# The third row pair of the gate and up weights in seven products, with one weight sum made by an adding DMA

## Chip, cores and metric

The kernel runs on one core of one Trainium2 chip. The metric is the device time of one execution in microseconds (us); of the kernel before it is 2270.07 us, the median of 3 runs (2270.04 to 2271.07).

## What is computed

A trunk of four pre-norm residual layers over 256 tokens of width 2048: a gated linear recurrence (HGRN2) or gated linear attention (GLA), each with cross-attention into 256 memory tokens and an output projection, and after each of the two a SwiGLU feed-forward layer. Everything is float32. The part around the change is the feed-forward layer, the largest by weights (D_FF is 5632):

```python
hn = _rmsnorm(h, norm_ffn[layer])
gate, up = jnp.split(hn @ w_gate_up[layer], 2, axis=-1)
h = h + (jax.nn.silu(gate) * up) @ w_down[layer]
```

## The kernel before

**Products.** A float32 product is made of two float32r parts of each factor: `split` (L276) writes a weight's high part with ScalarE (a rounded copy) and its low part, the rest, with VectorE. A "product" is then three matmuls of 128x512 into one PSUM bank: high x high, high x low, low x high.

**Row pairs and kinds.** The 2048 rows of a weight are 8 row pairs of 2 x 128 rows. For a pair and two blocks of 512 columns (in the feed-forward layer one of gate and one of up) there are four weight tiles, two rows by two columns, and the 256 tokens are two halves of 128. So each pair is a 2 x 2 block product. A pair's kind says how it is made:

- `S` (`seven`, L420): seven products in the manner of Strassen and Winograd, 21 matmuls. It needs weight sums on VectorE, and parts of four sums beside those of three tiles: parts `a` (one tile of 512), `b`, `c` and `d` (two tiles, 1024, each).
- `O`: eight products, 24 matmuls, on the four weight tiles as they are (parts `a` and `b`) and on differences of the token factors.
- `H`: eight products, 24 matmuls, with the token factors that `S` has; it needs one weight difference and its parts.

The token factors are made once in each layer, in `Forms` (L359), by the kind of the pair in `PAIRS` (L354): "S" pairs get eight of them, "O" six. `project_halves` (L591) goes through the eight pairs of a block of gate and up columns with the kinds of `KINDS` (L1161). There are 11 such blocks a layer; the blocks 0 to 3 have rows of their own there and the blocks 4 to 10, here called steady, the last row. The same `load_pair` and `seven` serve the "S" pairs of the other projections (`project_two`, L516, for the memory keys and values, HGRN2, GLA, the output projection and the last two quads of the down weights).

**Order of work.** Between two gate/up blocks run two pieces of the down projection (`fd` in the profile), each over two quads (four row tiles, one load of 1024 KB each). The weights go through `raw` tiles of four 128x512 slots, with 3 buffers (`new_raw`, L271), loaded by SyncE's DMA queue in the order of use; a load waits until the last reader of the tile three before it, as a rule VectorE's last low part, is done. The parts go through tiles of tag `parts` with 6 buffers: an `S` pair takes three of them and one of tag `part`, an `O` pair or a quad two. So VectorE can work ahead of TensorE by that much. From the fourth pair of each layer's first gate/up block on, the instructions of TensorE, VectorE and ScalarE are kept in the order in which the program issues them (`Engine.kept`); `mark` and `due` put the sums of the last block, the gate and the transposes at fixed places in it. In each block of the feed-forward layer but the first, one low part of the down weights is written by GpSimd in place of VectorE (`free_port`, L286).

**An `S` pair on VectorE.** The low parts of `a` and `b`, then one sum of 1024 columns and two of 512, then the low parts of `c` and `d`. TensorE uses them in the order that the lists in `project_halves` give (`(1, 3, 2, 5, 7, 6, 4)`, and in the block's last pair `(1, 2, 6, 7, 5, 4, 3)`): product 1 is of `a`, 2 and 3 of `b`, 5 and 7 of `c`, 6 and 4 of `d`.

In the profile nearly every instruction of TensorE, VectorE and ScalarE has line L151, a helper that issues it, so that one reads by the tiles: `raw` (weights as loaded, and their sums), `parts143d` (parts d of raw tile 143), `f_p` (banks of a gate/up block), `fd` (banks of the down projection), `hf_7h` and `hf_7l` (token factors of pair 7, high and low). The three matmuls of a product with one stationary factor appear as a row of x2 (high factor) and one of x1 (low factor).

Of the kernel before, what the change touches and what calls it, by code (L numbers as in the profile page):

```python
# [17 lines left out]
P = 128  # L18
# [22 lines left out]
def trunk_kernel(ctx: ExitStack, tc: tile.TileContext, x, mem, norm_mix, norm_ffn, norm_mem,  # L41
# [234 lines left out]
    def split(src, name, by=2):  # L276
# [6 lines left out]
        for k in range(0, n, by):  # L283
            j = min(k + by, n)
            ac.copy(out=both[:, 0, k:j, 0:m], in_=src[:, k:j, :])
# [68 lines left out]
    PAIRS = "SSOSSOSB"  # L354
# [4 lines left out]
    class Forms:  # L359
# [20 lines left out]
        def put(self, ps, gains):  # L380
# [11 lines left out]
            if self.kind == "O":  # L392
# [3 lines left out]
            ve.scalar_tensor_tensor(out=g[:, 4, :], in0=g[:, 0, :], scalar=-1.0, in1=g[:, 3, :],  # L396
                                           op0=ALU.mult, op1=ALU.subtract)
            tt(out=g[:, 5, :], in0=g[:, 1, :], in1=g[:, 0, :], op=ALU.subtract)
            tt(out=g[:, 6, :], in0=g[:, 3, :], in1=g[:, 5, :], op=ALU.subtract)
            tt(out=g[:, 7, :], in0=g[:, 2, :], in1=g[:, 6, :], op=ALU.subtract)  # L400
# [7 lines left out]
    def load_pair(raw, w, p, c0, c1, n):  # L408
# [7 lines left out]
        for j, c in ((slice(0, 4, 3), c0), (slice(1, 3), c1)):  # L416
            nc.sync.dma_start(out=raw[:, j, 0:n],
                              in_=w[2 * p * P:(2 * p + 2) * P, c:c + n].rearrange("(k p) c -> p k c", p=P))

    def seven(i, raw, between=None):  # L420
# [8 lines left out]
        tt(out=raw[:, 0:2, :], in0=raw[:, 0:4:2, :], in1=raw[:, 1:2, :].broadcast_to([P, 2, n]), op=ALU.subtract)  # L429
        tt(out=raw[:, 2, :], in0=raw[:, 2, :], in1=raw[:, 0, :], op=ALU.add)  # L430
        tt(out=raw[:, 3, :], in0=raw[:, 3, :], in1=raw[:, 2, :], op=ALU.subtract)
        t5, t7 = split(raw[:, 0:2, :], f"{i}c")
        t6, t4 = split(raw[:, 2:4, :], f"{i}d")
        return {1: ("x00", b00), 2: ("x01", b10), 3: ("z", b11), 4: ("x11", t4), 5: ("s", t5), 6: ("u", t6), 7: ("d0", t7)}

    def further(g):

        tt = ve.tensor_tensor
        ve.scalar_tensor_tensor(out=g[:, 4, :], in0=g[:, 1, :], scalar=-1.0, in1=g[:, 3, :], op0=ALU.mult, op1=ALU.subtract)
        tt(out=g[:, 5, :], in0=g[:, 0, :], in1=g[:, 1, :], op=ALU.subtract)  # L440
        tt(out=g[:, 6, :], in0=g[:, 3, :], in1=g[:, 5, :], op=ALU.subtract)
        tt(out=g[:, 7, :], in0=g[:, 2, :], in1=g[:, 6, :], op=ALU.subtract)
# [73 lines left out]
    def project_two(pairs, plan, w, c0, c1, n, name, give, view=lambda ps: ps, onto=None, prep=None, behind=None,  # L516
# [43 lines left out]
        for at, (p, kind) in enumerate(zip(order, plan)):  # L560
            i, raw = new_raw()
            if i == 0:
                load_pair(raw, w, p, c0, c1, n)
            if prep:
                prep(at)
            if i > 0:
                load_pair(raw, w, p, c0, c1, n)
            if kind == "S":
                todo = held(behind, seven, i, raw[:, :, 0:n]) if behind else seven(i, raw[:, :, 0:n])
                last = at == plan.rindex("S")  # L570
                for b in (1, 6, 7, 5, 2, 4, 3) if last else (3, 2, 1, 5, 7, 6, 4):
# [817 lines left out]
```

## Time and profile before

| | |
|---|---|
| median of 3 runs | 2270.07 us |
| the profiled execution's own time | 2271.69 us |
| its span, first to last instruction | 2269.9 us |
| granted TensorE clock | 0.999 |
| TensorE busy | 2250.8 us |
| VectorE busy | 2065.8 us |
| ScalarE busy | 1423.5 us |
| GpSimd busy | 83.4 us |
| moved by DMA | 435.78 MB |

The profile is of one execution. PE is TensorE, DVE VectorE, ACT ScalarE, POOL GpSimd, SP SyncE with its DMA queue. A row of a group of instructions has: line, engine, operation, output and inputs by tile, shapes and type, count; behind the first bar the busy time in us and the mean of one in ns; behind the second the idle time of the engine before them, and who ended it. A window's row has, for each engine, the busy time in it and the number of instructions, then the granted clock, the share of time in which the DMA engines were busy, and GB/s.

### The profile page before, as it was taken

What the parts mean: (1) busy time and instruction counts of PE and PEld (TensorE: products, weight loads), DVE (VectorE), ACT (ScalarE), POOL (GpSimd) and SP (SyncE); (2) the same over time, 40 slices, a digit from 0 to 9 for tenths busy, and PEclk for the clock granted to TensorE, in tenths of its full rate; (3) what the DMA queues carried; (4) which work ended last, traced back from release to release, by engine and by line L of the source; (5) the groups of instructions that cost most, each with busy time, mean ns of one, the idle gap of its engine ahead of it and who ended that gap; (6) DMA issues with size and microseconds to landing.
All of it is one profiled execution on the core that took longest, in us unless ns stands there. A gap on an engine that the chain in (4) does not pass through costs nothing.

```text
span 2269.9 us, 29374 instructions
## 1 busy us (share of the span) xinstructions
PE 2250.8 (99%) x10710; PEld 1901.4 (84%) x10710; DVE 2065.8 (91%) x2615; ACT 1423.5 (63%) x1938; POOL 83.4 (4%) x61
## 2 busy tenths in 40 slices
PE   9999999999999999999999999999999999999998
PEld 7888888888888888888889999988888888888887
DVE  7889999899999999999996887899899999999997
ACT  6655656566666666666665665566566666666664
POOL 0000000000000000000000000001000000000000
PEclk9999999999999999999999999999999999999999
DMA  8645545455556665555665446555556565665564
GB/s 289 204 151 183 186 157 177 167 168 203 170 202 222 204 206 190 203 199 204 204 212 174 142 146 190 157 176 203 197 194 203 205 210 194 205 205 202 205 217 153
DMA packets 232644, 435.78 MB, mean 192 GB/s; under 512 B 13199, under 2 KB 42675, under 8 KB 232243
## 3 DMA queue, kind: packets, MB, share of 16 engines
q1 hardware_dynamic: 231203, 429.64, 56.4%
q10 hardware_dynamic: 1296, 4.26, 0.5%
q8 instruction: 84, 1.38, 0.2%
q14 instruction: 61, 0.50, 0.1%
HBM read 430.71 MB, written 3.15 MB: 191 GB/s over the span
## 4 chain that ended last, share of the span: by engine, by line
PE 89%; DVE 6%; ACT 2%; issue 1%; DMA 1%; POOL 0%; SPq 0%; POOLq 0%; DVEq 0%; ACTq 0%
PE f_p L151 39%; PE fd L151 19%; PE wo L151 4%; PE m1p L151 2%; PE wo0p L151 2%; PE hf0p L151 2%; PE wo1p L151 2%; PE fd_0p L151 2%; PE gk1p L151 1%; PE gg11p L151 1%; PE gg10p L151 1%; PE gg01p L151 1%; PE m0p L151 1%; DVE raw L151 1%; PE gx L151 1%
## 5 line engine op out<-in xcount | busy, mean ns | idle before, releaser
L151 DVE TENSOR_TENSOR raw<-raw 128x512 f32<-128x512 f32 (+3 forms) x474 | 403.6, 852 | 9.2
L151 ACT CAST parts<-raw 128x1024 fp32r<-128x1024 f32 (+1 forms) x216 | 212.0, 1016 | 44.6 <-DMA raw<-in_w_down_dram 9.8
L151 DVE TENSOR_TENSOR parts<-raw,parts 128x1024 fp32r<-128x1024 f32 (+1 forms) x196 | 224.0, 1180 | 15.2 <-ACT parts L151 15.1
L286 POOL TENSOR_TENSOR parts<-raw,parts 128x1024 fp32r<-128x1024 f32 x20 | 48.2, 2411 | 1187.1 <-ACT parts L151 1138.6
L151 ACT COPY h<-fd 128x512 f32<-128x512 f32 x80 | 46.3, 588 | 55.0 <-PE fd L151 52.1
L151 ACT ACTIVATE s<-s,rf_r 128x512 f32<-128x512 f32 x44 | 31.8, 722 | 41.6 <-DVE s L151 41.4
L151 DVE TENSOR_TENSOR e<-f_p,e 128x512 f32<-128x512 f32 x66 | 45.2, 685 | 2.3
L151 ACT COPY fd<-h 128x512 f32<-128x512 f32 x82 | 45.2, 582 | 0.0
L151 PE MATMUL fd<-parts,s_6h 128*128 128x512 f32 x128 | 39.8, 392 | 0.0
L151 PE MATMUL fd<-parts,s_8h 128*128 128x512 f32 x128 | 39.8, 392 | 0.0
L151 PE MATMUL fd<-parts,s_4h 128*128 128x512 f32 x128 | 39.8, 392 | 0.0
L151 PE MATMUL fd<-parts,s_2h 128*128 128x512 f32 x128 | 39.8, 392 | 0.0
L151 PE MATMUL fd<-parts,s_0h 128*128 128x512 f32 x128 | 39.8, 392 | 0.0
L151 PE MATMUL fd<-parts,s_5h 128*128 128x512 f32 x128 | 39.4, 389 | 0.0
L151 PE MATMUL fd<-parts,s_3h 128*128 128x512 f32 x128 | 39.4, 389 | 0.0
L151 PE MATMUL fd<-parts,s_7h 128*128 128x512 f32 x128 | 39.4, 389 | 0.0
L151 PE MATMUL fd<-parts,s_1h 128*128 128x512 f32 x128 | 39.4, 389 | 0.0
L151 DVE TENSOR_TENSOR s<-f_p,e 128x512 f32<-128x512 f32 x44 | 30.3, 689 | 4.3 <-PE f_p L151 2.4
L151 DVE SCALAR_TENSOR_TENSOR s<-e,rf_r,s 128x512 f32<-128x512 f32 x44 | 31.0, 747 | 0.2
L151 PEld LDWEIGHTS fd<-parts,s_7h 128*128 128x128 f32 x128 | 24.0, 188 | 5.0
L151 PEld LDWEIGHTS fd<-parts,s_3h 128*128 128x128 f32 x128 | 24.0, 188 | 5.0
L151 PEld LDWEIGHTS fd<-parts,s_1h 128*128 128x128 f32 x128 | 24.0, 188 | 5.0
(5723 smaller groups left out, 7258.1 us busy)
## 6 DMA issues: line engine op xcount, KB each, us to landing
raw<-in_w_gate_up_dram SPq DMA_DIRECT2D x352, 512.0 KB, 3.9
raw<-in_w_down_dram SPq DMA_DIRECT2D x80, 1024.0 KB, 5.7
raw<-in_hgrn_w_in_dram SPq DMA_DIRECT2D x96, 512.0 KB, 3.9
raw<-in_gla_w_in_dram SPq DMA_DIRECT2D x96, 384.0 KB, 3.3
raw<-in_w_out_dram SPq DMA_DIRECT2D x16, 1024.0 KB, 5.8
raw<-in_w_out_dram SPq DMA_DIRECT2D x32, 512.0 KB, 4.1
raw<-in_w_mem_kv_dram SPq DMA_DIRECT2D x30, 512.0 KB, 5.5
raw<-in_w_down_dram SPq DMA_DIRECT2D x16, 512.0 KB, 4.1
```

The lines of the kernel that those rows point to most:

```text
L151: ins = func(*args, **kwargs)
L286: low = (nc.gpsimd if free_port else ve).tensor_tensor(out=both[:, 1, k:j, 0:m], in0=src[:, k:j, :], in1=both[:, 0, k:j, 0:m].bitcast(F32) ...
```

## The change

In steady blocks pair 2 becomes an `S` pair (`PAIRS` and the last row of `KINDS`): seven `S` and one `O` in place of six and two. As its token factors are now those of `S`, it becomes `H` in the blocks 0 to 3 of each layer, where it was `O`.

In all `S` pairs of the kernel, the weight sum of slot 1 (the upper row's second column block plus the lower row's) is no longer made by VectorE: after the two loads of the pair, which change places, GpSimd issues a DMA that reads the lower row's tile (128x512, or 128x384 in GLA) from DRAM once more and adds it onto slot 1 (`accum_op=ALU.add`). There are 168 of these. The signs of the sums change to suit: VectorE then makes one sum of 512 columns and one of 1024, parts `c` are now those of the products 6 and 7 and are written negated (`turned`: ScalarE's copy with scale -1, VectorE's low part by a scalar_tensor_tensor), parts `d` are those of 5 and 4. The token sums (`Forms.put`, `further`) change sign alike, and the order of the products becomes `(1, 3, 2, 6, 7, 5, 4)`; in the last pair it stays as it was in numbers, but 6 is now of `c` and 5 of `d`. The diff:

```diff
--- before.py
+++ after.py
@@ -273,7 +273,7 @@
         n_w[0] += 1
         return i, wts.tile([P, 4, 512], F32, tag="raw", name=f"raw{i}", bufs=3)
 
-    def split(src, name, by=2):
+    def split(src, name, by=2, turned=False):
 
         n, m = src.shape[1:]
         if n == 1:
@@ -282,6 +282,12 @@
             both = wts.tile([P, 2, 2, 512], F32R, tag="parts", name=f"parts{name}", bufs=6)
         for k in range(0, n, by):
             j = min(k + by, n)
+            if turned:
+                hi = both[:, 0, k:j, 0:m]
+                ac.activation(out=hi, in_=src[:, k:j, :], func=AF.Copy, scale=-1.0)
+                ve.scalar_tensor_tensor(out=both[:, 1, k:j, 0:m], in0=src[:, k:j, :], scalar=-1.0, in1=hi.bitcast(F32),
+                                        op0=ALU.mult, op1=ALU.subtract)
+                continue
             ac.copy(out=both[:, 0, k:j, 0:m], in_=src[:, k:j, :])
             low = (nc.gpsimd if free_port else ve).tensor_tensor(
                 out=both[:, 1, k:j, 0:m], in0=src[:, k:j, :], in1=both[:, 0, k:j, 0:m].bitcast(F32), op=ALU.subtract)
@@ -351,7 +357,7 @@
 
 
 
-    PAIRS = "SSOSSOSB"
+    PAIRS = "SSSSSOSB"
     HOMES = (("hq", "hq"),) * 4 + (("F", "K"), ("T", "sc"), ("Q", None), ("v", "gate"))
     FACTORS = {"S": ("x10", "x00", "x01", "x11", "s", "d0", "u", "z"), "O": ("x10", "x00", "x01", "x11", "d0", "d1"),
                "B": ("x10", "x00", "x01", "x11", "s", "d0", "u", "z", "d1")}
@@ -393,11 +399,10 @@
                 tt(out=g[:, 4:6, :], in0=g[:, 1:3, :], in1=g[:, 0:4:3, :], op=ALU.subtract)
                 parts(0, 0, 6)
                 return
-            ve.scalar_tensor_tensor(out=g[:, 4, :], in0=g[:, 0, :], scalar=-1.0, in1=g[:, 3, :],
-                                           op0=ALU.mult, op1=ALU.subtract)
-            tt(out=g[:, 5, :], in0=g[:, 1, :], in1=g[:, 0, :], op=ALU.subtract)
-            tt(out=g[:, 6, :], in0=g[:, 3, :], in1=g[:, 5, :], op=ALU.subtract)
-            tt(out=g[:, 7, :], in0=g[:, 2, :], in1=g[:, 6, :], op=ALU.subtract)
+            tt(out=g[:, 4:6, :], in0=g[:, 3:0:-2, :], in1=g[:, 0:1, :].broadcast_to([P, 2, P]), op=ALU.subtract)
+            ve.scalar_tensor_tensor(out=g[:, 6, :], in0=g[:, 3, :], scalar=-1.0, in1=g[:, 5, :],
+                                    op0=ALU.mult, op1=ALU.subtract)
+            tt(out=g[:, 7, :], in0=g[:, 2, :], in1=g[:, 6, :], op=ALU.add)
             parts(0, 0, 8)
             if self.kind == "B":
                 tt(out=g[:, 4, :], in0=g[:, 2, :], in1=g[:, 3, :], op=ALU.subtract)
@@ -405,7 +410,7 @@
 
     TIMES = {"S": (1,) * 7, "O": (0, 2, 2, 2, 2, 0, 0), "H": (0, 2, 2, 2, 1, 0, 1)}
 
-    def load_pair(raw, w, p, c0, c1, n):
+    def load_pair(raw, w, p, c0, c1, n, kind):
 
         if n_w[0] == 1:
             for k, j, c in ((0, 0, c0), (0, 1, c1), (1, 3, c0), (1, 2, c1)):
@@ -413,9 +418,11 @@
                 if k == 0 and c == c1:
                     load_mem(0, 256, 512)
             return
-        for j, c in ((slice(0, 4, 3), c0), (slice(1, 3), c1)):
+        for j, c in ((slice(1, 3), c1), (slice(0, 4, 3), c0)):
             nc.sync.dma_start(out=raw[:, j, 0:n],
                               in_=w[2 * p * P:(2 * p + 2) * P, c:c + n].rearrange("(k p) c -> p k c", p=P))
+        if kind == "S":
+            nc.gpsimd.dma_start(out=raw[:, 1, 0:n], in_=w[(2 * p + 1) * P:(2 * p + 2) * P, c1:c1 + n], accum_op=ALU.add)
 
     def seven(i, raw, between=None):
 
@@ -426,20 +433,19 @@
         if between:
             between()
 
-        tt(out=raw[:, 0:2, :], in0=raw[:, 0:4:2, :], in1=raw[:, 1:2, :].broadcast_to([P, 2, n]), op=ALU.subtract)
-        tt(out=raw[:, 2, :], in0=raw[:, 2, :], in1=raw[:, 0, :], op=ALU.add)
-        tt(out=raw[:, 3, :], in0=raw[:, 3, :], in1=raw[:, 2, :], op=ALU.subtract)
-        t5, t7 = split(raw[:, 0:2, :], f"{i}c")
-        t6, t4 = split(raw[:, 2:4, :], f"{i}d")
+        tt(out=raw[:, 0, :], in0=raw[:, 1, :], in1=raw[:, 0, :], op=ALU.subtract)
+        tt(out=raw[:, 2:4, :], in0=raw[:, 2:4, :], in1=raw[:, 0:1, :].broadcast_to([P, 2, n]), op=ALU.subtract)
+        t6, t7 = split(raw[:, 0:2, :], f"{i}c", turned=True)
+        t5, t4 = split(raw[:, 2:4, :], f"{i}d")
         return {1: ("x00", b00), 2: ("x01", b10), 3: ("z", b11), 4: ("x11", t4), 5: ("s", t5), 6: ("u", t6), 7: ("d0", t7)}
 
     def further(g):
 
         tt = ve.tensor_tensor
-        ve.scalar_tensor_tensor(out=g[:, 4, :], in0=g[:, 1, :], scalar=-1.0, in1=g[:, 3, :], op0=ALU.mult, op1=ALU.subtract)
+        tt(out=g[:, 4, :], in0=g[:, 3, :], in1=g[:, 1, :], op=ALU.subtract)
         tt(out=g[:, 5, :], in0=g[:, 0, :], in1=g[:, 1, :], op=ALU.subtract)
-        tt(out=g[:, 6, :], in0=g[:, 3, :], in1=g[:, 5, :], op=ALU.subtract)
-        tt(out=g[:, 7, :], in0=g[:, 2, :], in1=g[:, 6, :], op=ALU.subtract)
+        ve.scalar_tensor_tensor(out=g[:, 6, :], in0=g[:, 3, :], scalar=-1.0, in1=g[:, 5, :], op0=ALU.mult, op1=ALU.subtract)
+        tt(out=g[:, 7, :], in0=g[:, 2, :], in1=g[:, 6, :], op=ALU.add)
 
     class Pair:
 
@@ -560,15 +566,15 @@
         for at, (p, kind) in enumerate(zip(order, plan)):
             i, raw = new_raw()
             if i == 0:
-                load_pair(raw, w, p, c0, c1, n)
+                load_pair(raw, w, p, c0, c1, n, kind)
             if prep:
                 prep(at)
             if i > 0:
-                load_pair(raw, w, p, c0, c1, n)
+                load_pair(raw, w, p, c0, c1, n, kind)
             if kind == "S":
                 todo = held(behind, seven, i, raw[:, :, 0:n]) if behind else seven(i, raw[:, :, 0:n])
                 last = at == plan.rindex("S")
-                for b in (1, 6, 7, 5, 2, 4, 3) if last else (3, 2, 1, 5, 7, 6, 4):
+                for b in (1, 6, 7, 5, 2, 4, 3) if last else (3, 2, 1, 6, 7, 5, 4):
                     product(b, pairs[p].get(todo[b][0]), todo[b][1])
                 if last and at == len(plan) - 1:
                     early()
@@ -607,12 +613,12 @@
         for p, kind in enumerate(kinds):
             Engine.kept = keep <= p
             i, raw = new_raw()
-            load_pair(raw, w, p, c0, c1, 512)
+            load_pair(raw, w, p, c0, c1, 512, kind)
             x = forms[p].get
             last = p == len(PAIRS) - 1
             if kind == "S":
                 todo = seven(i, raw, lambda: mark(key + p))
-                for b in (1, 2, 6, 7, 5, 4, 3) if last else (1, 3, 2, 5, 7, 6, 4):
+                for b in (1, 2, 6, 7, 5, 4, 3) if last else (1, 3, 2, 6, 7, 5, 4):
                     product(b, x(todo[b][0]), todo[b][1])
             else:
                 b00, b01 = split(raw[:, 0:2, :], f"{i}a")
@@ -1158,7 +1164,7 @@
     PARTS = ((0,), (1, 2), (3, 4), (5, 6), (7, 8), (9, 10))
 
 
-    KINDS = ("SHOSHOSO", "HHOSSOSO", "SHOSSOSO", "SSOSSOHS", "SSOSSOSS")
+    KINDS = ("SHHSHOSO", "HHHSSOSO", "SHHSSOSO", "SSHSSOHS", "SSSSSOSS")
```

In the program, 42 of 8304 matmuls of 128x512 go. Three places show how the rows move (line, operation, output and inputs with the program's own numbers, shape, count).

VectorE, the last pair of a steady block, raw tile 143 (`parts143a` to `parts143d`; `raw_...` is the tile itself), before:

```order
L151 TENSOR_TENSOR parts143a<-raw_6748,parts143a 128x512
L151 TENSOR_TENSOR parts143b<-raw_6748,parts143b 128x1024
L151 TENSOR_TENSOR raw_6748<-raw_6748 128x1024
L151 TENSOR_TENSOR raw_6748<-raw_6748 128x512 x2
L151 TENSOR_TENSOR parts143c<-raw_6748,parts143c 128x1024
L151 TENSOR_TENSOR parts143d<-raw_6748,parts143d 128x1024
```

and after:

```order
L151 TENSOR_TENSOR parts143a<-raw_6772,parts143a 128x512
L151 TENSOR_TENSOR parts143b<-raw_6772,parts143b 128x1024
L151 TENSOR_TENSOR raw_6772<-raw_6772 128x512
L151 TENSOR_TENSOR raw_6772<-raw_6772 128x1024
L151 SCALAR_TENSOR_TENSOR parts143c<-raw_6772,parts143c 128x1024
L151 TENSOR_TENSOR parts143d<-raw_6772,parts143d 128x1024
```

One sum of 512 columns is gone, the sum of 512 columns stands ahead of that of 1024, and the low part of `c` has another operation.

TensorE, the same pair (`f_5_p_...` are the block's banks), from its first product on, before:

```order
L151 MATMUL f_5_p_6492<-parts143a,hf_7h 128x512 x2
L151 MATMUL f_5_p_6492<-parts143a,hf_7l 128x512
L151 MATMUL f_5_p_6500<-parts143b,hf_7h 128x512 x2
L151 MATMUL f_5_p_6500<-parts143b,hf_7l 128x512
L151 MATMUL f_5_p_6512<-parts143d,hf_7h 128x512 x2
L151 MATMUL f_5_p_6512<-parts143d,hf_7l 128x512
L151 MATMUL f_5_p_6508<-parts143c,hf_7h 128x512 x2
L151 MATMUL f_5_p_6508<-parts143c,hf_7l 128x512
```

and after:

```order
L151 MATMUL f_5_p_6510<-parts143a,hf_7h 128x512 x2
L151 MATMUL f_5_p_6510<-parts143a,hf_7l 128x512
L151 MATMUL f_5_p_6518<-parts143b,hf_7h 128x512 x2
L151 MATMUL f_5_p_6518<-parts143b,hf_7l 128x512
L151 MATMUL f_5_p_6522<-parts143c,hf_7h 128x512 x2
L151 MATMUL f_5_p_6522<-parts143c,hf_7l 128x512
L151 MATMUL f_5_p_6526<-parts143c,hf_7h 128x512 x2
L151 MATMUL f_5_p_6526<-parts143c,hf_7l 128x512
L151 MATMUL f_5_p_6530<-parts143d,hf_7h 128x512 x2
L151 MATMUL f_5_p_6530<-parts143d,hf_7l 128x512
```

The first product on `d` comes after those on `a`, `b` and both on `c`; before, it came after those on `a` and `b`.

GpSimd's queue, from the end of one gate/up block (`raw_6250` and `raw_6289` are its pairs 6 and 7) over the low part of a down quad to the next steady block, after:

```order
L425 DMA raw_6250<-in_w_gate_up_dram 128x512
L425 DMA raw_6289<-in_w_gate_up_dram 128x512
L292 TENSOR_TENSOR parts_0_6376<-raw_6374,parts_0_6376 128x1024
L425 DMA raw_6492<-in_w_gate_up_dram 128x512
L425 DMA raw_6538<-in_w_gate_up_dram 128x512
L425 DMA raw_6583<-in_w_gate_up_dram 128x512
L425 DMA raw_6622<-in_w_gate_up_dram 128x512
L425 DMA raw_6661<-in_w_gate_up_dram 128x512
L425 DMA raw_6733<-in_w_gate_up_dram 128x512
L425 DMA raw_6772<-in_w_gate_up_dram 128x512
```

Before, only the rows of L286, now L292, stood here, one for each block. Each block's seven adding DMAs now stand between them, in the order of the pairs, and pair 0's stands behind the low part of the down quad.

## Prediction

> **What bounds the kernel now.** I read the page's first block first, for the share of each engine.
>
> ```profile
> span 2269.9 us, 29374 instructions
> PE 2250.8 (99%) x10710; PEld 1901.4 (84%) x10710; DVE 2065.8 (91%) x2615; ACT 1423.5 (63%) x1938; POOL 83.4 (4%) x61
> ```
>
> TensorE has 19 us idle in all, but VectorE is so full that its order could matter. So next the chain that ended last, in order of time (start, length, what), over one steady block and the start of the next.
>
> ```profile
> 736.42 39.65 PE f_p L151 x174
> 776.06 16.32 PE fd L151 x72
> 793.26 5.46 PE fd L151 x24
> 798.72 39.65 PE f_p L151 x174
> ```
>
> A block takes 798.72 - 736.42 = 62.30 us, all of it on TensorE. Its gate/up part is 174 products of 128x512 in 39.65 us: 0.2279 us each. Then the same block by engine:
>
> ```profile
> core 0: us, PE busy (x) PEld busy (x) DVE busy (x) ACT busy (x) POOL busy (x), PEclk, DMA share, GB/s
> 798.72:861.02 62.30, 62.30 (x279) 51.44 (x279) 59.37 (x65) 40.10 (x49) 2.42 (x1) 1.00 0.60 203
> ```
>
> TensorE is never idle and VectorE has 62.30 - 59.37 = 2.93 us left. How near VectorE is to being waited for shows at the block's last pair (raw 143), in the timelines of TensorE and VectorE:
>
> ```profile
> 833.91 0.62 PE L151 MATMUL f_p<-parts143b,hf_7h 128*128 128x512 f32 x2
> 834.60 0.78 PE L151 MATMUL f_p<-parts143d,hf_7h 128*128 128x512 f32 x2
> 833.60 1.23 DVE L151 TENSOR_TENSOR parts143d<-raw,parts143d 128x1024 fp32r<-128x1024 f32 x1
> ```
>
> The two products on 143d take 0.78 us where those on 143b take 0.62: VectorE writes its low part until 834.83, and the second product waits for it, some 0.1 us. TensorE bounds the block, with VectorE level with it at this place.
>
> **Fewer products.** In each of 14 steady blocks (7 in each layer) pair 2 makes 7 products of three matmuls instead of 8: 42 matmuls fewer, 42 x 0.2279 = 9.57 us. In the first four blocks of a layer pair 2 goes from kind O to kind H, 24 matmuls either way: nothing on TensorE.
>
> **VectorE in a steady block.** The durations, by form, and ScalarE's beside them:
>
> ```profile
> L151 DVE TENSOR_TENSOR parts<-raw,parts 128x1024 fp32r<-128x1024 f32 x180 | 212.7, 1222 | 3.7 <-ACT parts L151 3.7
> L151 DVE TENSOR_TENSOR raw<-raw 128x512 f32<-128x512 f32 x300 | 207.5, 692 | 8.4
> L151 DVE TENSOR_TENSOR raw<-raw 128x1024 f32<-128x1024 f32 x144 | 175.7, 1220 | 0.3
> L151 DVE SCALAR_TENSOR_TENSOR s<-e,rf_r,s 128x512 f32<-128x512 f32 x44 | 31.0, 747 | 0.2
> L151 ACT CAST parts<-raw 128x1024 fp32r<-128x1024 f32 x200 | 201.8, 1047 | 33.0 <-DMA raw<-in_w_down_dram 9.8 <-DMA raw<-in_w_out_dram 7.9 <-PE m1p L151 5.4
> L151 ACT ACTIVATE ab<-ab 128x1024 f32<-128x1024 f32 x4 | 4.2, 1061 | 0.1
> ```
>
> An S pair before: low parts a 0.69, b, c and d 1.22 each, sums 1.22 + 0.69 + 0.69, together 6.95 us. After: one 0.69 sum less (the DMA makes it), and c by a scalar_tensor_tensor, of which no row has this size. Lower bound 1.22, as if it were a tensor_tensor; upper bound 1.22 x 747/692 = 1.32; I take 1.28, that is 0.055 more, as for the row of 512. So 0.69 + 1.22 + 0.69 + 1.22 + 1.28 + 1.22 = 6.32. An O pair is 2 x 1.22 = 2.44. The block's eight pairs: before 6 x 6.95 + 2 x 2.44 = 46.6, after 7 x 6.32 + 2.44 = 46.7. What VectorE would have paid for the seventh S pair, the DMA pays. ScalarE gets 1.05 + 0.58 us more in a block and 0.014 for each turned copy, on 40.10 of 62.30: hidden.
>
> **The last pair, which is the place that could take the gain back.** TensorE reaches it 34.2 us into the block (150 matmuls) instead of 34.9 (153). It needed d after 6 of its matmuls (1.37 us) and c after 9; now, by the new order, c after 6 and d after 12 (2.73). Margins, from the -0.1 of before: d is needed 0.68 later (36.92 for 36.24) and ready 0.1 later, +0.5. c is needed at 35.56, 0.68 earlier than d was, and ready 46.6 - 45.5 = 1.1 earlier, +0.3. With c at 1.32 both lose 0.3 and stay at or above zero; with 1.22 both gain 0.4. So the 0.68 us per block stays, and TensorE is still what is late next. Earlier in the block five S pairs now follow each other, each 6.32 - 4.79 = 1.53 us behind; VectorE starts on pair 0 at 850.47 (the next rows) and TensorE at 798.72 + 62.30 = 861.02, a lead of 10.5 us. The fifth pair's c is ready 5 x 6.32 - 1.22 = 30.4 us after VectorE's start and needed at 10.5 + 4 x 4.79 + 9 x 0.2279 = 31.7. It holds.
>
> **The sum by DMA.** It must land before the first sum of its pair. Tightest is pair 0 of a block; VectorE's timeline there, then what lands how fast:
>
> ```profile
> 850.47 0.69 DVE L151 TENSOR_TENSOR parts148a<-raw,parts148a 128x512 fp32r<-128x512 f32 x1 [1.60 <-ACT parts148a L151]
> 852.57 1.95 DVE L151 TENSOR_TENSOR raw<-raw 128x1024 f32<-128x1024 f32 x2
> 843.09 6.70 SPq L417 DMA_DIRECT2D raw<-in_w_gate_up_dram  x6
> raw<-in_w_gate_up_dram SPq DMA_DIRECT2D x352, 512.0 KB, 3.9
> raw<-in_w_mem_kv_dram SPq DMA_DIRECT2D x4, 256.0 KB, 5.9
> out_dram<-h SPq DMA_DIRECT2D x4, 256.0 KB, 2.5
> ```
>
> The load that it adds to is issued at 843.09 (the third row merges six issues; now the first is this half) and lands 3.9 later, at 847.0. It is needed at 852.57: 5.6 us for issue on GpSimd, transfer and landing. The trace has no DMA of GpSimd's and none that adds; the nearest rows, 256 KB each, say 2.5 to 5.9 us. I take 4.2, the middle, since neither the quiet end of the kernel (2.5) nor its crowded start (5.9) is the place: 1.4 to spare. At 5.9 it is 0.3 late, which the margin of 0.3 takes. Other pairs have two or three pairs' work between load and sum, over 10 us. The Trainium skill (DMA: Bandwidth & Descriptors, Anatomy of one DMA) gives a DMA of GpSimd's 2.0 us plus its bytes at 436 GB/s, an estimate of 2.6 us; by that the time would be the same. On the GpSimd queue the issue of pair 0 stands behind the low part that GpSimd makes in the down blocks; that one ends by 840.5 (2.41 us from 838.06 on, the 2.42 of the window above), before the load is even issued. The swapped order of the two loads costs the c0 half 0.4 us, 7 us ahead of its use.
>
> **Elsewhere.** The S pairs outside the steady blocks lose 0.63 us of VectorE each, and where they stand three in a row TensorE waits for their last parts; the waits, in total:
>
> ```profile
> PE hv0p L151 <- ACT parts34d L151: 0.9, 1, 0.9
> PE hv1p L151 <- ACT parts50d L151: 0.7, 1, 0.7
> PE gg00p L151 <- DVE parts238d L151: 0.5, 1, 0.5
> PE hv2p L151 <- DVE parts65d L151: 0.5, 1, 0.5
> PE hf2p L151 <- DVE parts58d L151: 0.5, 1, 0.5
> PE hf1p L151 <- DVE parts42d L151: 0.4, 1, 0.4
> PE m0p L151 <- DVE parts6d L151: 0.3, 1, 0.3
> PE gg00p L151 <- ACT parts238d L151: 0.2, 1, 0.2
> ```
>
> They add up to 4.0 us. d comes over 1 us earlier and, in the last S pair, is needed after 9 matmuls instead of 3: I count 3 us as gone (bounds 0 and 4).
>
> **The sum.** The profiled execution took 2271.69 us (span 2269.9 and 1.8 around it), 1.6 above the median of the runs. 2271.69 - 9.57 - 3 = 2259.1; less the 1.6, against the median, 2257.5. With the bounds (0 to 4 us of waits; pair 0 up to 0.2 us beyond its margin, 14 times; a us of scatter, as the runs of before show from 2270.04 to 2271.07) its own range is 2255 to 2264.
>
> **Rivals.**
> 1. *The sum lands late.* Each us beyond pair 0's margin comes 14 times, because VectorE has nothing to do meanwhile and ends the block level with TensorE. If issue and transfer take 6.2 to 6.8 us, 0.3 to 0.9 over, 4 to 13 us come back: 2262 to 2270. For it: over 40 MB more traffic, just while pairs 1 and 2 load (all six issues within 6.7 us). Against: the DMA queues are busy 0.60 of the time. 0.17.
> 2. *GpSimd is kept from issuing.* This is the slow side. GpSimd can be held for a long run of VectorE's two-input work:
>
> ```profile
> 1576.38 9.30 POOL L189 TENSOR_TENSOR rf_r<-rf_v,mhalf 128x2 f32<-128x2 f32 x1 [82.98 <-DVE rf_v L151]
> 1576.38:1585.68 9.30, 9.30 (x47) 7.66 (x46) 9.30 (x16) 7.04 (x11) 9.29 (x1) 1.00 0.64 226
> L912 POOL MEMSET sch<- 128x1024 f32 x3 | 2.9, 956 | 224.3 <-PE po L151 96.1 <-DVE ro_v L151 95.4 <-PE ao L151 32.9
> L1112 POOL MEMSET gk<- 128x1024 f32 x1 | 1.0, 957 | 53.7 <-PE fd L151 53.7
> ```
>
>    Four numbers a partition took 9.30 us while VectorE was busy without a break. If the issue waits like that, it goes out only once VectorE itself stops for the sum, at 852.57, and lands 4.2 later: 4.2 - 0.3 = 3.9 us, 14 times, 55 us: 2312, and more if other pairs suffer. It decides from 1.2 us of lateness on (14 x 0.9 = 12.6, the whole gain). Against it: the four fills of 128x1024, which only write, took 956 and 957 ns wherever they fell, and an issue reads no tile. The Trainium skill (GPSIMD Engine Reference, Key points) says that GpSimd shares its SBUF interfaces with VectorE and contends with instructions of two SBUF inputs; the 9.30 us agree, the fills do not. 0.13.
> 3. *The turned low part runs at half speed.* c would be 2.44, 1.16 more in each S pair, 8.1 in a steady block: c 7.8 us late, 14 times, 109 us, near 2365. The Trainium skill (Vector Engine (DVE) Microarchitecture Reference, Points that are easy to get wrong) has this rule: a scalar_tensor_tensor with two SBUF sources that aren't bf16 halves its throughput. The row s<-e,rf_r,s is such a one, and its 747 ns against 692 speak against it. 0.04.
> 4. *The change does not take out what it says.* The matmuls of 128x512 fall by just 42 in the program, so no chance is left here.
>
> **How the numbers follow.** Forecast 0.66, rivals 0.17, 0.13 and 0.04. A measurement of this kernel can tell 0.2%, 4.5 us, which ends at 2265.5. The forecast lies beyond that, and of rival 1 a good third (0.07): faster 0.73, same 0.10, slower 0.13 + 0.04 = 0.17. The range takes the forecast's own and rival 1, and ends at 2271 for the us of scatter; it leaves out rivals 2 and 3.
>
> **What would show it.** Right: 171 products in a steady block, a block of about 61.6 us, scalar_tensor_tensor parts at 1.22 to 1.32 us, the added sums landing within 5.6 us of their load, and the waits for 34d to 238d gone. Wrong: VectorE idle before the first sum of pair 0 and TensorE waiting for the last pair's c or d (rival 1), the same with GpSimd's issue far behind the load's landing (rival 2), parts c near 2.4 us (rival 3).

## The result, and the profile after

The changed kernel takes 2322.11 us, median of 4 runs (2320.36 to 2328.36), beside 2270.57 (2270.04 to 2273.11) for the kernel before: ratio 1.023, 95% interval 1.0218 to 1.0242. It is slower by 51.5 us where some 13 us less was forecast. The profiled execution took 2323.37 us (span 2321.6); against the span of before that is 2321.6 - 2269.9 = 51.7 more.

The page of the changed kernel, its span, engines and DMA queues:

```profile
span 2321.6 us, 30266 instructions
...
PE 2262.7 (97%) x10668; PEld 1892.1 (82%) x10668; DVE 2035.3 (88%) x2525; ACT 1451.4 (63%) x1974; POOL 220.3 (9%) x229
...
q1 hardware_dynamic: 231203, 429.64, 55.3%
q0 software_dynamic: 24192, 43.40, 12.2%
```

The 42 matmuls are gone (10710 - 10668), and VectorE (DVE) has 30 us less work than before. Yet TensorE (PE) is now idle for 59 us of the span instead of 19. The new queue, q0, holds the adding DMAs: it takes 12.2 / 43.40 = 0.28% of the DMA engines per MB, where the loads on q1 take 55.3 / 429.64 = 0.13%. A byte that is added costs the DMA engines about twice what a byte that is loaded does.

Where the 51.7 us lie, read from TensorE's timeline as the time between the first products on two weight tiles, after less before: the stages up to the first gate and up block (HGRN2) -4.9; the first four gate and up blocks of both layers +7.1; the 14 steady blocks +36.5; the GLA stage +10.6; the down products behind layer 0's blocks +1.3; the end +1.1; the rest 0. So the steady blocks, which should have given 9.6, took most. One of them, by engine, from pair 0's first product to the next block's:

```profile
core 0: us, PE busy (x) PEld busy (x) DVE busy (x) ACT busy (x) POOL busy (x), PEclk, DMA share, GB/s
2206.58:2270.95 64.37, 62.48 (x276) 50.72 (x275) 58.21 (x65) 40.62 (x50) 7.60 (x7) 1.00 0.79 235
```

It takes 64.37 us for 62.30 before. What VectorE does at this block's pair 0 (raw 400) stands in its timeline (start, length, what; in brackets the idle time ahead of it and what ended that):

```profile
2196.20 0.69 DVE L151 TENSOR_TENSOR parts400a<-raw,parts400a 128x512 fp32r<-128x512 f32 x1 [0.41 <-ACT parts400a L151]
2197.15 1.23 DVE L151 TENSOR_TENSOR parts400b<-raw,parts400b 128x1024 fp32r<-128x1024 f32 x1 [0.26 <-ACT parts400b L151]
2201.24 1.95 DVE L151 TENSOR_TENSOR raw<-raw 128x512 f32<-128x512 f32 x2 [2.87 <-DMA raw<-in_w_gate_up_dram]
2203.12 1.23 DVE L151 SCALAR_TENSOR_TENSOR parts400c<-raw,parts400c 128x1024 fp32r<-128x1024 f32 x1
```

VectorE stands still for 2.87 us before the first sum, and a DMA of the weights ends the wait. The third and fourth rows answer two other questions: the sum of 512 columns is there, without the second one, and the turned low part `c` takes 1.23 us, no more than `b`. GpSimd's timeline (POOL) shows who issues that DMA and when:

```profile
2194.65 0.88 POOL L425 DMA_DIRECT2D raw<-in_w_gate_up_dram  x1 [7.31 <-DMA raw<-in_w_gate_up_dram]
2198.25 0.86 POOL L425 DMA_DIRECT2D raw<-in_w_gate_up_dram  x1 [2.71 <-DMA raw<-in_w_gate_up_dram]
```

GpSimd was waiting for the load, which was issued at 2189.99 and landed at 2194.0; it issues 0.65 us later. Nothing holds it. But the adding DMA lands at 2201.15, 6.5 us after that. Over this stretch (2189 to 2203), the DMA engines' busy tenths in 40 slices, and the queues:

```profile
DMA  2111149379999998938999998989999999999999
...
q1 hardware_dynamic: 1680, 3.24, 70.3%
q0 software_dynamic: 218, 0.41, 17.5%
```

Before the change the same place of a block (842 to 856 there) read:

```profile
q1 hardware_dynamic: 1688, 3.25, 69.3%
```

So the DMA engines are 88% busy there (70.3 + 17.5, the nines are full slices), while three pairs load at once; before, the loads alone took 69.3%. From the issue at 2194.65 until 2197.7 no packet of the adding DMA has started, and the loads have the DMA engines to themselves:

```profile
q1 hardware_dynamic: 461, 0.91, 93.8%
```

TensorE pays for it later. Its rows with a wait in that block:

```profile
2223.72 0.50 PE L151 MATMUL f_p<-parts403c,hf_3h 128*128 128x512 f32 x1 [0.43 <-DVE parts403c L151]
2229.74 0.50 PE L151 MATMUL f_p<-parts404c,hf_4h 128*128 128x512 f32 x1 [0.77 <-DVE parts404c L151]
2245.02 0.50 PE L151 MATMUL f_p<-parts407c,hf_7h 128*128 128x512 f32 x1 [0.70 <-DVE parts407c L151]
```

It does not wait for pair 0. It waits for `c` of pairs 3, 4 and 7: VectorE needs 6.3 us for an S pair and TensorE 4.8, so a delay at pair 0 shows only where VectorE's lead ends. The groups of VectorE by form name the whole:

```profile
L151 DVE TENSOR_TENSOR raw<-raw 128x512 f32<-128x512 f32 x178 | 122.5, 688 | 84.1 <-DMA raw<-in_w_gate_up_dram 62.7 <-issue 15.0 <-DMA raw<-in_hgrn_w_in_dram 3.1
```

84.1 us of idle time ahead of the first sums, where the kernel before had 8.4 in this group. All first sums together (the GLA stage has other shapes) lose 99 us to waits. The profile puts 76 of them down to a DMA; the others, too, end 0.08 us after an adding DMA has landed. In a steady block it is 2.86 us at pair 0 and 1.18 at pair 7 (means over the 14).

### The profile page after: what moved, and what is told of

Same layout as the page of the kernel before. It is cut to its first block, busy times and chain, and to the rows that moved or that the text cites. A ratio compares the mean times of both kernels' runs of the same rounds, so it can differ in the third digit from the quotient of the medians.

```text
span 2321.6 us, 30266 instructions
## 1 busy us (share of the span) xinstructions
PE 2262.7 (97%) x10668; PEld 1892.1 (82%) x10668; DVE 2035.3 (88%) x2525; ACT 1451.4 (63%) x1974; POOL 220.3 (9%) x229
## 3 DMA queue, kind: packets, MB, share of 16 engines
q1 hardware_dynamic: 231203, 429.64, 55.3%
q0 software_dynamic: 24192, 43.40, 12.2%
q8 instruction: 83, 1.36, 0.2%
## 5 line engine op out<-in xcount | busy, mean ns | idle before, releaser
L151 DVE TENSOR_TENSOR raw<-raw 128x512 f32<-128x512 f32 (+3 forms) x356 | 331.1, 930 | 104.8 <-DMA raw<-in_w_gate_up_dram 62.7
L151 DVE TENSOR_TENSOR parts<-raw,parts 128x1024 fp32r<-128x1024 f32 (+1 forms) x196 | 223.7, 1178 | 19.8 <-ACT parts L151 19.5
L425 POOL DMA_DIRECT2D raw<-in_w_gate_up_dram x128 | 110.9, 867 | 981.9 <-DMA raw<-in_w_gate_up_dram 624.8
L292 POOL TENSOR_TENSOR parts<-raw,parts 128x1024 fp32r<-128x1024 f32 x20 | 48.2, 2408 | 249.9 <-ACT parts L151 249.9
L425 POOL DMA_DIRECT2D raw<-in_hgrn_w_in_dram x17 | 14.8, 872 | 219.3 <-DMA raw<-in_hgrn_w_in_dram 110.4
```

The lines of the kernel that those rows point to most:

```text
L151: ins = func(*args, **kwargs)
L292: low = (nc.gpsimd if free_port else ve).tensor_tensor(out=both[:, 1, k:j, 0:m], in0=src[:, k:j, :], in1=both[:, 0, k:j, 0:m].bitcast(F32) ...
L425: nc.gpsimd.dma_start(out=raw[:, 1, 0:n], in_=w[(2 * p + 1) * P:(2 * p + 2) * P, c1:c1 + n], accum_op=ALU.add)
```

## The experiments

The theory from this profile: the adding DMA lands late at pairs 0 and 7, VectorE waits, and VectorE has no time left in these blocks to make up for it. Rivals: the adding DMAs' traffic slows all the loads; or VectorE and the new order cost more than was counted, sums or no sums. All runs are compared with the kernel before on the same chip (2270.1 to 2270.7).

**e_nosum: no adding DMA.** The sum is left out; everything else is the changed kernel.

```diff
-        if kind == "S":
-            nc.gpsimd.dma_start(out=raw[:, 1, 0:n], ..., accum_op=ALU.add)
```

> Leaves out the adding DMAs (slot 1 stays as loaded, so the weight sum is not made at all); all else as in the changed kernel. If the late sum is what costs (theory 1), or if the DMA's traffic is (theory 2), the time falls to what was predicted, 2256 to 2262 us, with steady blocks of about 61.6 us. If VectorE's new work or the new order is what costs (theory 3), it stays above 2300.

2254.01 us (2253.30 to 2254.24), ratio 0.9924 (0.9907 to 0.9940). A steady block, by engine:

```profile
2140.99:2202.40 61.41, 61.41 (x277) 50.94 (x275) 59.12 (x67) 43.21 (x54) 2.42 (x1) 1.00 0.61 209
```

TensorE is never idle in it. Fewer products, the turned parts and the new order give what they should: 0.86 us a block (mean 61.46 for 62.32), and 7.1 us up to the first gate and up block. All of the loss, 68 us, comes with the adding DMA.

**e_aside: the same DMAs, but nobody waits.** In the gate and up blocks the DMA adds to a tile that is never read, after the same load; the other projections keep theirs. The sum of these blocks is left out.

```diff
-            nc.gpsimd.dma_start(out=raw[:, 1, 0:n], ..., accum_op=ALU.add)
+            add = nc.gpsimd.dma_start(out=(aside[0] if aside else raw[:, 1])[:, 0:n], ..., accum_op=ALU.add)
```

> In the gate/up blocks the adding DMA goes out at the same point (after the first load of its pair has landed) with the same bytes, but adds onto a tile that nobody reads, so the weight sum is left out there; the other projections keep theirs. Theory 1 (waiting for the sum): steady blocks back to 61.6 us and, with GLA's 11 us still lost and HGRN2's 4 won, about 2265 us. Theory 2 (its traffic slows the loads): steady blocks stay at 63.5 us or more, 2295 to 2315.

2272.44 us (2269.27 to 2275.42), ratio 1.0006 (0.9996 to 1.0015). The total lies between the two forecasts, nearer to that of waiting, and the stages decide: the steady blocks take 61.58 us, 0.12 more than without any adding DMA, though all that traffic is there. One of them has seven issues of GpSimd (POOL) and the DMA share of the changed kernel, 0.79, and TensorE is not idle:

```profile
2157.01:2218.66 61.65, 61.65 (x277) 50.78 (x275) 54.76 (x61) 39.52 (x49) 7.60 (x7) 1.00 0.79 239
```

Of the 19.5 us by which its trace is longer than e_nosum's, 16 lie where the DMAs still add to the weights in use: 10.5 in the GLA stage, 2.4 behind layer 0's blocks, 3.2 at the end. The steady blocks have 1.7 of the rest and the first four blocks of the layers 1.9. So in the steady blocks it is the waiting, and the traffic by itself costs little.

**e_plain: the same DMA copies.** Same queue, same bytes, same wait, no addition; slot 1 is then the copied row and not the sum.

```diff
-            nc.gpsimd.dma_start(out=raw[:, 1, 0:n], ..., accum_op=ALU.add)
+            nc.gpsimd.dma_start(out=raw[:, 1, 0:n], ...)
```

> The same DMA from GpSimd with the same wait and bytes, but it copies where it added (the weight sum is left out). If it is the second transfer and its place behind the load that cost, whatever it does, landing stays near 4.6 us (6.5 at pair 0) and the time within 10 us of 2322. If adding itself makes the transfer slow, landing falls to about 3 us, pair 0's wait by 1.5 us or more, and the time to 2275 to 2300.

2270.52 us (2266.46 to 2277.32), ratio 0.9999 (0.9989 to 1.0008): just below the range that was given for a slow addition. The DMA queue and its issues (KB each, median us to landing):

```profile
q0 software_dynamic: 13280, 43.40, 6.1%
raw<-in_w_gate_up_dram POOLq DMA_DIRECT2D x128, 256.0 KB, 3.1
```

and in the changed kernel:

```profile
raw<-in_w_gate_up_dram POOLq DMA_DIRECT2D x128, 256.0 KB, 4.6
```

For the same bytes the addition doubles the time of the DMA engines (12.2% for 6.1%) and nearly doubles the packets (24192 for 13280), and the DMA lands 1.5 us later. By the packets' sizes, the copy's are of 4096 bytes and the adding DMA's of 2048, and one of either takes 0.21 us (means). Issue by issue: a copy lands after 2.9 us where next to nothing else loads (pair 2) and after 5.0 at pair 0; an adding DMA after 4.2 and 6.7. So of the 6.7 at pair 0 some 1.7 are the addition and 2.5 the loads beside it. Most of what the loads cost passes before the first packet: at pair 0 it starts 3.3 us after the issue (3.2 for a copy), at pair 3, where the loads take at most 7% of the DMA engines, after 1.6 (1.2 for a copy). The wait at pair 0 falls from 2.86 to 1.15, and the blocks to 62.02. The Trainium skill (DMA: Bandwidth & Descriptors, Anatomy of one DMA) gave an estimate of 2.6 us: near a copy that is alone, and short of the other three numbers, for which its sum has no term. The Trainium skill (Collectives: The Full Stack, Stop ④) calls the addition on the way through a DMA, in a collective's step, free; of VectorE's time that holds, and of the DMA engines' time it does not, by these rows.

**e_put0: other work of VectorE into the wait.** The two low parts of a down block that VectorE makes in pair 1 (`s_6l`, 1.3 us) are due in pair 0 instead.

```diff
-            dict(sums=10, gate=11, turn=((13, 101), (13, 101)), back=(13, 101)))
+            dict(sums=10, gate=11, turn=((13, 100), (13, 100)), back=(13, 101)))
```

> The four low and high parts of the last block's output (1.36 us on VectorE) are made in pair 0, between its low parts and its first sum, where VectorE now waits 2.7 us, and not in pair 1. Theory 1: 16 blocks win up to 1.36 us each, about 2322 - 19 = 2303 us, and VectorE's wait at pair 0 falls by 1.4. Theory 2: no more than 3 us either way.

2333.13 us (2325.36 to 2337.25), ratio 1.0269 (1.0245 to 1.0292): slower still, where 2303 was expected. VectorE's timeline at a pair 0:

```profile
2008.73 1.23 DVE L151 TENSOR_TENSOR parts364b<-raw,parts364b 128x1024 fp32r<-128x1024 f32 x1 [0.25 <-ACT parts364b L151]
2013.10 1.29 DVE L151 TENSOR_TENSOR s_6l<-tp_s_6h,s_6h 128x512 fp32r<-128x512 f32 x2 [3.14 <-ACT s_6h L151]
2014.31 1.94 DVE L151 TENSOR_TENSOR raw<-raw 128x512 f32<-128x512 f32 x2
```

and TensorE's, where the input of `s_6l` comes from:

```profile
2011.84 1.03 PE L151 MATMUL tp_s_6h<-ident,s 128*128 128x128 f32 x8
```

The moved work was not there to be done. It needs a turn on TensorE, which comes at 2011.84, so VectorE waits for that instead (3.03 us, mean) and does the 1.3 us later. The wait for the DMA is gone and the time is not, so this run does not tell the theories apart; it only shows that other waits at this place cost alike.

**e_kinds: the kinds alone, all sums by VectorE.** The kernel before, with only PAIRS and KINDS of the change.

```diff
-    PAIRS = "SSOSSOSB"
+    PAIRS = "SSSSSOSB"
-    KINDS = ("SHOSHOSO", "HHOSSOSO", "SHOSSOSO", "SSOSSOHS", "SSOSSOSS")
+    KINDS = ("SHHSHOSO", "HHHSSOSO", "SHHSSOSO", "SSHSSOHS", "SSSSSOSS")
```

> The kernel before with only the new kinds of pairs: a third S pair in the steady blocks (and H for O in the first four blocks of a layer), all three sums of an S pair by VectorE as before, no adding DMA. If VectorE's time in a steady block is what the adding DMA was there to save: VectorE has about 59 us of work in a block of e_nosum and gets one sum of 0.69 us more in each of seven S pairs, 4.8 us, so 64 us of work in a block where TensorE needs 61.4; blocks of 64 to 66 us, 14 of them, 2295 to 2325 us, with TensorE waiting for the low parts of pairs 3 to 5 and no wait of VectorE for a DMA. If VectorE had room for these sums all along (rival): blocks of 61.4 to 62.3 and 2258 to 2271 us.

2366.04 us (2364.98 to 2366.95), ratio 1.0417 (1.0402 to 1.0433): VectorE has no room for these sums, and the time is 41 us above the range. Its steady blocks take 68.21 us, where 64 to 66 was expected. At the start of a block, VectorE and then ScalarE (ACT):

```profile
2031.98 0.69 DVE L151 TENSOR_TENSOR parts364a<-raw,parts364a 128x512 fp32r<-128x512 f32 x1 [3.17 <-ACT parts364a L151]
```

```profile
2030.16 1.27 ACT L151 COPY h<-fd 128x512 f32<-128x512 f32 x2 [3.36 <-PE fd L151]
2031.33 0.62 ACT L151 CAST parts364a<-raw 128x512 fp32r<-128x512 f32 x1
```

What the expectation left out is, as I read these rows, a loop: TensorE, made late by VectorE, ends the down products late; ScalarE's two copies of them stand ahead of pair 0's high part in its queue; VectorE waits 3.17 us for that high part (2.81 on the mean, where e_mix below has 0.64) and falls behind again. No run takes this loop out.

**e_dmaonly: the DMA sums alone.** The changed kernel with PAIRS and KINDS of before (the two lines above, turned round).

> The changed kernel with the kinds of pairs of before: no product less, every S pair's one sum by the adding DMA. Theory: VectorE's waits for the late sum (about 2.7 us at pair 0 and 1.2 at pair 7 of a steady block) stay, but VectorE has 6 x 0.69 = 4 us less work in a block than before and an O pair to catch up in, so the wait at pair 0 goes under and only that at pair 7 can show: steady blocks of 62.3 to 63.3 us; the stages outside the steady blocks as in the changed kernel (about +12 us in all); 2278 to 2295 us. If each wait costs its full length whatever else VectorE has to do (rival): blocks of 66 us and 2325 or more.

2276.52 us (2272.32 to 2280.09), ratio 1.0022 (1.0013 to 1.0032), a little under the forecast's range and far from the rival's. Its steady blocks take 62.09 us, 0.2 less than before, with the adding DMA as slow as in the changed kernel (6.7 us at pair 0). A pair 0 on VectorE:

```profile
2028.76 0.69 DVE L151 TENSOR_TENSOR parts376a<-raw,parts376a 128x512 fp32r<-128x512 f32 x1 [3.02 <-ACT parts376a L151]
2029.70 1.23 DVE L151 TENSOR_TENSOR parts376b<-raw,parts376b 128x1024 fp32r<-128x1024 f32 x1 [0.26 <-ACT parts376b L151]
2030.85 1.95 DVE L151 TENSOR_TENSOR raw<-raw 128x512 f32<-128x512 f32 x2
```

Here VectorE is ahead, waits 3.02 us for ScalarE (and so for TensorE) before it starts the pair, and the sum has landed by the time it is wanted. Where some waits are left (0.6 at pair 0, 0.5 at pair 4, 0.8 at pair 7, on the mean), they cost nothing, since VectorE has 4 us less to do. A late sum costs time only where VectorE has none to spare. What this kernel loses lies in the GLA stage, 14.1 us.

**e_first: the slot to be added to is loaded first.** In S pairs a transfer of 256 KB of its own.

```diff
+        if kind == "S":
+            for j in (1, 2):
+                nc.sync.dma_start(out=raw[:, j, 0:n], in_=w[(2 * p + j - 1) * P:(2 * p + j) * P, c1:c1 + n])
-        for j, c in ((slice(1, 3), c1), (slice(0, 4, 3), c0)):
+        for j, c in ((slice(1, 3), c1), (slice(0, 4, 3), c0))[kind == "S":]:
```

> The changed kernel, but in S pairs the slot to which the DMA adds is loaded first, by a transfer of its own of 256 KB, then the slot beside it, then the other two: the adding DMA can start once 256 KB have landed instead of 512. Theory (the sum is late because load, issue and adding transfer come one after another): the load lands about 1 us earlier, the wait at pair 0 falls from 2.7 to about 1.7 us and with it each steady block by about 1 us; 2300 to 2312 us. If the adding transfer ends when the loads beside it end, whatever its start (rival): no change, 2318 to 2326.

2302.82 us (2299.48 to 2303.94), ratio 1.0137 (1.0122 to 1.0152). The wait at pair 0 falls to 1.37 us and the block to 63.65; the time is within the forecast. The adding DMA takes about as long as ever there (6.5 for 6.7), so it ends earlier because it starts earlier: load, issue and addition stand in a row, and that row is too long. At pair 7 it becomes slower (6.9 for 4.8), and the wait there grows from 1.18 to 1.36.

**e_hold: fewer loads beside pair 0's adding DMA.** In the steady blocks pair 1's loads, and those behind them, wait until it has landed.

```diff
+            while first_add:
+                tc.add_manual_dep(load.ins, first_add.pop().ins.name, ..., reason="hold")
```

> The changed kernel, but in the steady blocks the loads of pair 1 (and with them those of pair 2, behind it on the same queue) wait until pair 0's adding DMA has landed: that DMA then runs with no load beside it. If the loads beside it make it slow (6.5 us and more at pair 0, where the quiet ones take 4.15): it lands about 4.2 us after its issue, VectorE's wait at pair 0 falls from 2.7 us to under 0.6, and a wait of 1 to 2 us comes up at pair 1, whose load and sum now start later; blocks of 63.5 to 65 us, 2300 to 2322. If an adding DMA at pair 0 is slow by itself (rival): it still takes 6 us, the wait at pair 0 stays at 2.7, pair 1's comes on top, 2335 or more.

2359.18 us (2351.61 to 2366.84), ratio 1.0392 (1.0370 to 1.0414). By its time that is the rival's case; by its waits it is not. VectorE in a block's first two pairs:

```profile
2027.65 1.95 DVE L151 TENSOR_TENSOR raw<-raw 128x512 f32<-128x512 f32 x2 [1.46 <-DMA raw<-in_w_gate_up_dram]
...
2039.30 0.69 DVE L151 TENSOR_TENSOR raw<-raw 128x512 f32<-128x512 f32 x1 [4.21 <-DMA raw<-in_w_gate_up_dram]
```

Pair 0's adding DMA now lands after 5.08 us (mean) instead of 6.71, and its wait falls to 1.16. Other loads still run beside it: from its issue to its landing the loads take 36% of the DMA engines, where they took 76%. So the loads beside it do slow it, though 4.2 was expected. The time is lost at pair 1: held back, its adding DMA meets the loads that were held, takes 6.9, and makes VectorE wait 4.0 us, where 1 to 2 was expected.

**e_mix and e_mix07: the DMA only where there is time.** VectorE makes the sum in pairs 0, 6 and 7 (e_mix) or 0 and 7 (e_mix07) of the gate and up blocks, and in all projections behind the first of these blocks.

```diff
-        if kind == "S":
+        if kind == "S" and by_dma[0]:
+            added.add(n_w[0] - 1)
...
+        if i not in added:
+            tt(out=raw[:, 1, :], in0=raw[:, 1, :], in1=raw[:, 2, :], op=ALU.add)
...
+            by_dma[0] = 0 < p < 6
```

(the last line is `0 < p < 7` in e_mix07.)

> The changed kernel, with the adding DMA only where the sum has time: in pairs 1 to 5 of the gate and up blocks and in the projections ahead of the first gate and up block. In pairs 0, 6 and 7 and in all later projections VectorE makes that sum too (0.69 us each). Theory: no wait for a late sum is left; the GLA stage is as before (10.6 us less than in the changed kernel), the HGRN2 stage 5 to 7 us shorter than before; VectorE has 59 + 3 x 0.69 = 61 us of work in a steady block, level with TensorE's 61.4: blocks of 61.5 to 63; 2254 to 2275 us. If the traffic of the adding DMAs, not their lateness, costs the time (rival): at least 2290.

> As e_mix, but pair 6 too has its sum from the adding DMA: VectorE makes it in pairs 0 and 7 of the gate and up blocks only. If a steady block's length is VectorE's (60.7 us and every sum that it makes itself or every us that it waits): 0.69 us less in each of 14 blocks than in e_mix, 62.1 us, and 2266 us (2263 to 2269). If the block is TensorE's (rival): no change against e_mix, 2274 to 2277.

e_mix: 2275.66 us (2274.58 to 2276.84), ratio 1.0021 (1.0011 to 1.0031), just above its range, and far from the rival's 2290. No wait for a sum is left in the steady blocks, the GLA stage is as before, and a block takes 62.82. e_mix07: 2273.01 us (2270.09 to 2274.67), ratio 1.0011 (1.0002 to 1.0020). Its blocks are 62.21 us, 0.61 shorter for one sum of 0.69 less, as the theory had it; but of these 8.5 us in 14 blocks 3.4 went again in the first four blocks and 1.2 at the end, and the total missed 2266 by 7. A block of it by engine:

```profile
2155.82:2218.15 62.33, 61.75 (x276) 50.87 (x275) 60.02 (x70) 41.02 (x52) 5.01 (x4) 1.00 0.70 226
```

**e_old_kinds: the part of the change that pays.** e_dmaonly, with VectorE's own sums in the projections behind the first gate and up block (`by_dma` as in e_mix, but with the adding DMA in all `S` pairs of the gate and up blocks).

> As e_dmaonly (the kinds of pairs of before, no product less), with the adding DMA only in the gate and up blocks and in the projections ahead of them; in the GLA stage and later VectorE makes that sum. Theory: e_dmaonly lost 14 us in the GLA stage alone and nothing in the steady blocks, so this gives 2276.5 - 14.1 - 0.5 = 2262 us (2259 to 2266), below the kernel before, which has the same products. Rival (the waits in the steady blocks cost something there too): 2268 or more.

2262.28 us (2261.13 to 2264.77), ratio 0.9968 (0.9956 to 0.9980): below the kernel before by 7.8 us, with the same products. Up to the first gate and up block it gains 7.1, in the steady blocks 2.6, in the GLA stage 0.4 (by its trace).

**All of it on one line.** e_mix makes three of the sums and waits for none, so its block says what VectorE needs without them: 62.82 - 3 x 0.69 = 60.75 us (its small idle times between instructions among it). For the other kernels with the new kinds, 60.75 and their sums and waits in a steady block (means), beside the measured length:

| kernel | sums of its own and waits, us | 60.75 + these | measured block |
|---|---|---|---|
| e_nosum | 0 | 60.75 | 61.46 (TensorE) |
| e_mix07 | 1.38 | 62.13 | 62.21 |
| e_plain | 1.15 + 0.23 | 62.13 | 62.02 |
| e_first | 1.37 + 1.36 | 63.48 | 63.65 |
| the changed kernel | 2.86 + 1.18 | 64.79 | 64.93 |
| e_put0 | 3.03 + 0.14 + 1.31 | 65.23 | 65.66 |
| e_hold | 1.16 + 4.00 + 1.07 | 66.98 | 67.39 |

To within 0.45 us, every us that VectorE waits or works beyond 0.7 lengthens the block by a us, whichever pair it falls in. The waits counted are those for a DMA and e_put0's for `s_6h`. e_kinds comes near the line only when its longer wait for ScalarE is counted too: 60.75 + 7 x 0.69 + 2.81 - 0.64 = 67.75, beside 68.21.

## Why the prediction was wrong

**The step that failed is the sum by DMA**: "I take 4.2, the middle", with ends of 2.5 and 5.9, against 5.6 us to spare. Three things in it were off, all to one side.

1. *Its length.* 4.2 us is right for an adding DMA that is alone (4.05 to 4.6 at pair 2), without the 0.65 that pass before its issue. At pair 0 it is 0.65 and 6.71 on the mean (5.89 to 7.96), beyond my upper end. I had rows of loads and of a store, none of which adds, and the "against" of rival 1 was the mean of a whole block, 0.60 busy; the stretch in question had 69.3% before the change, with full slices in it, and 88% after. The place should have been read, not the block.
2. *The time to spare.* 5.6 us held 1.60 of VectorE's idling for ScalarE (`148a`). That was slack, and not fixed: once VectorE is behind, it does not idle there (0.41 at `400a`), and the sum is wanted 4.4 us after the load, at 2201.24 - 2.87 = 2198.37. So the DMA is 2.8 late where its length alone (0.65 + 6.50 in this block) would say 1.6.
3. *The other pairs.* "Over 10 us" between load and sum holds for pairs 1 to 3 alone. From the adding DMA's issue to the time when its sum is wanted there are, on the mean, 8.4 us at pair 4, 5.5 at pair 6 and 3.7 at pair 7. At pairs 4 and 6 that is enough (the DMA takes 5.2 and 4.2). At pair 7 it takes 4.8, beside the down loads, and VectorE waits 1.18. The GLA stage (+10.6) and the first four blocks (7.1 where e_nosum has 1.2) were given no term for a late sum.

With the measured waits, the prediction's way of counting gives the steady blocks: 14 x (2.86 + 1.18 less the 0.7 that VectorE has left) = 46.8 us over e_nosum, where 48.6 were measured. The rest of the way from e_nosum's span of 2252.0 to 2321.6 is measured and not worked out: GLA 10.6, the first blocks 5.9, the stages before them 2.2, the others 2.3.

**Rival 1 was the case.** It had the mechanism and the price ("because VectorE has nothing to do meanwhile"), 14 us for each us of lateness in a block: 3.3 us beyond the margin make 47. Its sizes were too small. It was given 6.2 to 6.8 us for issue and transfer, and 7.4 came; and with its margin of 5.9 those 7.4 would have cost only 1.5 x 14 = 21 us, since it knew neither of the idle time that goes nor of pair 7. So it ended slower than before and not within it; that side had been left to rivals 2 and 3.

**Right.** The 42 matmuls (the prediction's 174 and 171 "products" of a block are matmuls): 0.86 us a block without the sums, 0.68 of them from three matmuls. The rest I put down to the last pair, where the 0.1 us waits went: e_dmaonly, with no matmul less, gained 0.2. The margins at the last pair and at the fifth S pair hold in e_nosum, where TensorE never waits in the steady blocks. `c` takes 1.23, at the lower end of 1.22 to 1.32, so rival 3 is out: the rule of the Trainium skill that was cited for it (Vector Engine (DVE) Microarchitecture Reference, Points that are easy to get wrong) does not show here, where it would have been 2.44. Rival 2 is out too: in the steady blocks GpSimd issues 0.56 to 0.92 us after the load has landed, where the profile tells the landing, each issue takes 0.86 to 0.90, and VectorE's two-input work around it does not hold it. The waits for 34d to 65d in the HGRN2 stage go: 4.9 us less up to the first gate and up block in the changed kernel, 7.1 without its late sums, for 3 forecast. That is more than all the waits that the prediction lists (4.0), so its size is partly luck; what else became shorter there is open.

**Open.** Of the 6.7 us at pair 0, 1.7 are the addition (copy against sum, 5.0 and 6.7) and 1.6 the loads that e_hold moved away; it was not tried with the c0 half of its own pair and the down loads moved too. That its first packet starts late beside loads is in the records; why, no run shows. That the GLA stage's 10.6 us come from its adding DMAs was shown by taking them out (0.0 in e_nosum, -0.1 in e_mix, -0.4 in e_old_kinds); which of its waits make them was not taken apart, nor why the same stage lost 14.1 in e_dmaonly.

## What to carry to other kernels

Work that is handed from a busy engine to a DMA is not free if that engine waits for it: count load, issue and transfer as one row, at the busy share of the DMA queues in that very stretch, and ask what idle time the waiting engine has there once it is behind. A price per us is worth more than a guess of the us: here a us of VectorE's time in a block was 14 us of the kernel, so a term with ends of 2.5 and 5.9 us and no row of its kind should have put more weight on the slow side. When a change does two things, try each alone: the sums by DMA in the gate and up blocks and ahead of them, with the old kinds, gave 0.3% (ratio 0.9968, 0.9956 to 0.9980), and the new kinds, once VectorE made the two sums that come too late, gave blocks of the same length (62.2 us for 62.1).

## What the runs showed of the hardware

An adding DMA from HBM to SBUF (256 KB, 128x512 f32, issued by GpSimd) lands 4.2 us after its issue when alone and 6.7 beside loads that fill the DMA engines, where a copy of the same bytes takes 2.9 and 5.0. It takes 12.2% of the DMA engines over the kernel where the copy takes 6.1%: its packets are half as large (2048 bytes for 4096), and each takes as long (0.21 us). GpSimd spends 0.87 us on each issue of an adding DMA and 0.54 on that of a copy (e_plain). Beside loads, the first packet starts 3.3 us after the issue instead of 1.6. A scalar_tensor_tensor of 128x1024 with two f32 inputs in SBUF takes VectorE 1.23 us, as a tensor_tensor does.
